# Two-layer streaming encoder on one core: more modulation vectors by selector products, and layer 0's last piece and short conv laid out anew

## The chip, the core and the metric

The program runs on one core of one Trainium2 chip, in one launch. The metric is device time in microseconds (us) of that launch. Engines are named as in the profile: PE (TensorE matmul) and PEld (its weight loads), DVE (VectorE), ACT (ScalarE), POOL (GpSimd), SP (SyncE, which here only issues transfers). Each engine runs its own list of instructions; waits between engines are semaphores.

## The reference, cut to what matters

256 tokens of width 2048 pass two layers, in float32. Each layer is

```
mod = silu(c) @ w_mod[l] + b_mod[l]            # six vectors of 2048: shift, scale, gate; twice
h = layer_norm(x) * (1 + scale_m) + shift_m
proj = h @ w_in[l]                             # 4288 columns, four head groups
y = concat(gmlp, latent attention, short conv, conformer conv) @ w_out[l]
x = layer_norm(ALPHA * x + (1 + gate_m) * y, post_mix_g[l], post_mix_b[l])
h = layer_norm(x) * (1 + scale_f) + shift_f
x = layer_norm(ALPHA * x + (1 + gate_f) * conv_ffn(h), post_ffn_g[l], post_ffn_b[l])
```

The weights w_mod, w_in, w_out, w_up and w_down are read once each; that is most of the 601 MB that the page shows as read.

## The kernel before, in words

**Tiles.** Tokens are two tiles of 128 (t0, t1; in the trace x0 and x1), the model width is 16 tiles of 128 (kt). A weight arrives as a raw tile of 1 MB (`rawp`, four buffers). Most products are done in three passes: ACT rounds the weights to a high part (`whi`, L455), DVE makes the low part (`wlo`, L456), the activations are split likewise, and PE adds high x high, high x low and low x high. The halves live in `splitp`: four buffers for high, four for low. Other products use the float32 weights as they are (`wexact`, loaded straight into buffers of `splitp` or into a slot); the trace shows two PE records for each of these. Every matmul is issued by the helper at L83.

**Modulation.** The six vectors of a layer are sums over 16 row tiles of w_mod, made on DVE: `mod_step` (L245, executed as L248 and L250) multiplies a tile by a column of silu(c) and adds it into `macc`. These steps run in the background, paced by the products (`mod_stream`, `pump`). A finished `macc` still has to be summed over its 128 partitions. For a gate this is `gate_rows` (L283). For a shift or scale there are two ways. `mod_cols` (L198) takes 128 columns of `macc` as PE's weights against one column of ones: a matmul with one output column for each of up to 16 tiles, all in float32, then one ACT instruction (L207 or L86). `mod_rows` (L220) splits `macc` into high and low parts on ACT and DVE (`mhi`, `mlo`; `halves`, L214, from the buffers of `splitp`), multiplies them by selector matrices of four columns, 512 columns at a time (`ps_row`), copies the four rows to SBUF on ACT (`mrow`, L227), transposes them on PE in four instructions (L230), and adds the bias on DVE (L232, tile `mod`). `settle` (L299) chooses: before, `mod_rows` for layer 1's shift_f and scale_f, `mod_cols` for the rest. Of layer 0's shift_f and scale_f the last 4 of 16 column tiles are summed apart, later (`LATE_KT` = 12).

**Output projections and norms.** `out_proj` (L663) serves w_out (tiles o) and w_down (tiles d). It goes over the output columns in chunks of 1024, 512 and 512. Of the last chunk the last four units of weights are held back, and `done` (L832) multiplies them for t0 and then for t1. Then it calls `before()`, which settles the shift and scale that the next norm needs (`needs`, L1499), and then `finish` for t0 (L701 yg, L704 x, L707 statistics), `second` (the norm of t0), and the same for t1 with `norm`. `first_group` (L613) then transposes the normed tile on PE (L594, ps_xT), applies scale and shift, and begins the next products with t0 alone, then t1. The tiles o_153600 and o_153610 are w_out's last chunk for t0 and t1; d_153600 and d_153610 the same for w_down of layer 0.

**Layer 0's mixers.** `by_pieces` (L1250) goes over the 16 kt in five pieces, because layer 0's own shift and scale become known piece by piece. In each, products for the groups D (conformer conv), U and V (gMLP), E (short conv's gate) are made, D in four parts between the others. After the last piece (kt 12 to 15) come `mix_d` (which queues 31 taps of a depthwise conv as background work: four ACT products and one DVE add, L910, for a tap), `mix_v` (gMLP's norm and mixing, tiles va, mixed, ya), group B with `mix_b` (the attention: tiles kvr, ps_rkv, qc, ps_sc, p, ps_pT) and group C (the short conv, tiles C_c). B and C use `wexact` throughout.

**Order.** The instructions are written in the program's order and then placed on each engine by a scheduler; the order that results is fixed when the program is built.

Of the kernel before, what the change touches and what calls it, by code (L numbers as in the profile page):

```python
# [8 lines left out]
F32R = mybir.dt.float32r  # L9
AF = mybir.ActivationFunctionType  # L10
# [3 lines left out]
P = 128  # L14
# [4 lines left out]
KT = D // P  # L19
# [35 lines left out]
def encoder_kernel(ctx: ExitStack, tc: tile.TileContext, A: dict, consts: bass.AP, out: bass.AP):  # L55
# [26 lines left out]
    def mm(o, lhsT, rhs, start, stop):  # L82
        pe.matmul(o, lhsT, rhs, start=start, stop=stop, skip_group_check=True)  # L83
# [127 lines left out]
            MOD[(l, m, k0 + j)] = cols[:, j : j + 1]  # L211
            MOD_BY[(l, m, k0 + j)] = done.ins.name

    def halves(acc, c0):  # L214
        hi = splitp.tile([P, 1024], F32R, tag="whi", name="mhi")
        lo = splitp.tile([P, 1024], F32R, tag="wlo", name="mlo")
        split((hi, lo), acc[:, c0 : c0 + 1024])
        return [(hi[:, i * 512 : (i + 1) * 512], lo[:, i * 512 : (i + 1) * 512]) for i in range(2)]

    def mod_rows(l, m, acc):  # L220

        ps = ms_tile("ps_row")
        for j, pair in enumerate(halves(acc, 0) + halves(acc, 1024)):
            for n, part in enumerate(pair):
                mm(ps[0:4, :], onesR[:, P + 4 * j : P + 4 * j + 4], part, j + n == 0, j + n == 4)
        row = tmp_tile("mrow")
        act.copy(row[0:4, :], ps[0:4, :])  # L227
        ps = ms_tile("ps_mod")
        for i in range(4):
            pe.transpose(ps[:, 4 * i : 4 * i + 4], row[0:4, i * P : (i + 1) * P], ident[0:4, 0:4])  # L230
        cols = keep.tile([P, KT], F32, name=f"mod_{l}_{m}")
        done = dve.scalar_tensor_tensor(  # L232
            out=cols.rearrange("p (i j) -> p i j", i=4),
            in0=ps[:, 0:KT].rearrange("p (i j) -> p i j", i=4),
            scalar=0.0 if m == SHIFT_F else 1.0,
            in1=bcol[l][:, m * KT : (m + 1) * KT].rearrange("p (j i) -> p i j", i=4),
            op0=ALU.add,
            op1=ALU.add,
        )
        for k in range(KT):  # L240
# [58 lines left out]
    def settle(i=0):  # L299
        l, m, acc, k0, k1 = late.pop(i)  # L300
        if m in (GATE_M, GATE_F):
            gate_rows(l, m, acc)
        elif (l, m) in ((1, SHIFT_F), (1, SCALE_F)):
            mod_rows(l, m, acc)
        else:
            mod_cols(l, m, k0, acc[:, k0 * P : k1 * P])

# [165 lines left out]
    def split(dst, src):  # L473
        hi, lo = dst[:2]
        act.copy(hi, src)  # L475
        dve.tensor_tensor(out=lo, in0=src, in1=hi.bitcast(F32), op=ALU.subtract)  # L476

    def group(w, c0, width, name, then, ntm=0, nk=2, hF=None, bg=0, spare=0, begun=None):

        ncm = (width - 512 * ntm) // P
        box = {}

        skip = 0 if begun is None else PLAIN_KT // nk

        def products(item, u):
            if u == skip:
                box["c"] = [acc_tile(f"{name}_c{i}") for i in range((ncm + 1) // 2)]
                if begun is not None:  # L490
                    for bank, part in zip(box["c"], begun):
                        act.copy(bank, part)
                box["t"] = [[acc_tile(f"{name}_t{t}{i}") for i in range(ntm)] for t in range(2)]
                box["h"] = list(hT)
            for part in (range(0, min(4, ncm)), range(4, ncm)):
                for k, (hi, lo) in enumerate(item):
                    kt = u * nk + k
                    st, sp = kt == 0, kt == KT - 1
                    for i in part:
                        o = box["c"][i // 2][:, (i % 2) * S : (i % 2 + 1) * S]  # L500
                        off = slice(i * P, (i + 1) * P)
                        first = st and i % 2 == 0
                        if lo is None:
                            mm(o, hi[:, off], hF(kt), first, sp)
                        else:
                            xh, xl = (h[:, kt % 2, :] for h in box["h"][kt // 2][:2])
                            mm(o, hi[:, off], xh, first, False)
                            mm(o, hi[:, off], xl, False, False)
                            mm(o, lo[:, off], xh, False, sp)
            for k, (hi, lo) in enumerate(item):  # L510
                kt = u * nk + k
                st, sp = kt == 0, kt == KT - 1
                for i in range(ntm):
                    off = slice(ncm * P + i * 512, ncm * P + (i + 1) * 512)
                    for t in range(2):
                        tok = slice(t * P, (t + 1) * P)
# [344 lines left out]
    def mixers(l, w_in, Y, hF=None, between=None):  # L861
# [102 lines left out]
                    func=AF.Gelu_apprx_tanh,  # L964
                )

        def mix_v(_, tps):
            ua = Y["a"]
            if l == 0:
                ga, gb = act_tile("gmlp0"), act_tile("gmlp1")  # L970
            else:
# [10 lines left out]
            va = slot("va").rearrange("p (t c) -> p t c", t=2)  # L982
            for t in range(2):
                act.activation(out=va[:, t, :], in_=tps[t][0], func=AF.Gelu_apprx_tanh)
# [5 lines left out]
            pool.memset(wT[64:128, :, 0:64], 0.0)  # L990
            for t in range(2):
# [239 lines left out]
                )  # L1231

        if hF is not None:
            return by_pieces(l, w_in, hF, between, mix_d, mix_u, mix_v, mix_b, mix_c, mix_e)
# [12 lines left out]
        run(group(w_in, C_SB, 512, f"E{l}", mix_e, nk=4, bg=STEPS[l]["E"]))  # L1247
        drain_background()

    def by_pieces(l, w_in, hF, between, mix_d, mix_u, mix_v, mix_b, mix_c, mix_e):  # L1250


        hf = lambda kt: hF[kt // 4][:, kt % 4, :]
# [49 lines left out]
        for q, (k0, nkt) in enumerate(PIECES):  # L1303
# [22 lines left out]

            turns_d = [(kt, h) for kt in range(k0, k0 + nkt) for h in range(2)]
            n = len(turns_d) // 4
            for s in range(4):
                mine = turns_d[s * n : (s + 1) * n]  # L1330
                if ("D", mine[0][0]) not in loaded:
                    load("D", mine[0][0])
                some_mods((0.3, 0.7, 1.0, 1.0)[s])
                if s == 3 and ahead[1] is not None:
                    ahead[1]()
                for kt, h in mine:
                    d_part(kt, h)
                for g in ("U", "VB", "E", "")[s] if exact else ("U", "V", "E", "")[s]:
# [3 lines left out]
                if k0 + nkt == KT:  # L1342
                    if s < 3:
                        next(mods)
                    if s > 0:
                        turns.pop(0)()
                    if s == 3:
                        turns.pop(0)()
# [270 lines left out]
```

## Time and profile before

| What | Value |
|---|---|
| Median of 3 runs | 2282.78 us (2282.72 to 2288.62) |
| Profiled execution, its own time | 2281.42 us |
| Its span, first to last instruction | 2279.7 us |
| PE, DVE, ACT busy | 98%, 78%, 48% of the span |
| Mean granted PE clock | 0.991 |
| DVE's busy tenths, layer 0's mixers | 7 to 9 |
| End of layer 0's attention and short conv, first product of w_out | 313.68 us |
| First transposes after w_out and after w_down of layer 0 | 417.94 and 1191.44 us |

A row of a timeline gives start, duration, engine, line, operation, output and inputs, and in brackets how long the engine had been idle and for whom. A row of windows gives for a stretch the busy time of PE, PEld, DVE, ACT and POOL with the count of instructions, then the granted PE clock as a fraction of full speed.

### The profile page before, as it was taken

How to read it: one execution, taken by the hardware profiler on the slowest of the kernel's cores; microseconds unless marked ns; L12 is line 12 of the kernel's file. 1: busy time of each engine (PE TensorE's matmuls, PEld its weight loads, DVE VectorE, ACT ScalarE, POOL GpSimd, SP SyncE). 2: the span in 40 equal slices, each digit the busy share in tenths (PEclk: the TensorE clock that was granted, in tenths of full speed). 3: DMA queues.
4: the chain of work that ended last, by engine and by line, in shares of the span. 5: the costliest groups of instructions: out<-in, count | busy, mean ns of one | idle time of the engine just before them, and what ended most of it. 6: DMA issues, size and time to landing. Idle time of an engine off the chain costs nothing.

```text
span 2279.7 us, 31503 instructions
## 1 busy us (share of the span) xinstructions
PE 2238.7 (98%) x12387; PEld 1934.8 (85%) x12387; DVE 1773.3 (78%) x2183; ACT 1098.2 (48%) x1644; POOL 35.1 (2%) x65
## 2 busy tenths in 40 slices
PE   7999999999999999999999999999999999999998
PEld 5788886798888888888789999889888888888886
DVE  5778988888888888988977899787676565565776
ACT  3356641354455444544454434545544454454553
POOL 0011000000000000000000000000000000000000
PEclk9999999999999999999999999999999999999999
DMA  9999699778888888898777677775666555555554
GB/s 349 385 373 359 256 328 349 249 278 314 311 307 315 314 312 327 303 346 302 273 236 254 201 242 250 271 273 177 240 240 215 192 185 197 191 185 194 187 191 148
DMA packets 228717, 605.21 MB, mean 265 GB/s; under 512 B 14660, under 2 KB 27188, under 8 KB 210900
## 3 DMA queue, kind: packets, MB, share of 16 engines
q1 hardware_dynamic: 227784, 602.30, 74.3%
q8 instruction: 97, 1.59, 0.3%
q0 software_dynamic: 784, 0.90, 0.1%
q14 instruction: 52, 0.43, 0.0%
HBM read 601.05 MB, written 2.10 MB: 265 GB/s over the span
## 4 chain that ended last, share of the span: by engine, by line
PE 88%; DVE 7%; DMA 2%; ACT 2%; issue 1%; POOL 0%; SPq 0%; DVEq 0%; ACTq 0%; POOLq 0%
PE g_c L83 22%; PE v_c L83 22%; PE d L83 20%; PE o L83 7%; PE D_c L83 3%; PE C_c L83 3%; PE B_c L83 2%; PE U_c L83 1%; PE E L83 1%; PE E_c L83 1%; DVE wlo L456 1%; PE ps_mod L83 1%; PE V L83 1%; DVE qacc L250 1%; DVE macc L250 1%
## 5 line engine op out<-in xcount | busy, mean ns | idle before, releaser
L455 ACT CAST whi<-wraw 128x1024 fp32r<-128x1024 f32 (+1 forms) x632 | 643.4, 1043 | 753.1 <-PE g_c L83 217.0
L456 DVE TENSOR_TENSOR wlo<-wraw,whi 128x1024 fp32r<-128x1024 f32 (+1 forms) x632 | 750.5, 1214 | 294.3 <-ACT whi L455 273.2
L83 PE MATMUL d<-whi,a 128*128 128x512 f32 x1344 | 390.3, 391 | 0.9 <-ACT whi L455 0.9
L250 DVE SCALAR_TENSOR_TENSOR macc<-wmod,cact,macc 128x2048 f32<-128x2048 f32 (+2 forms) x174 | 353.9, 2034 | 41.5 <-DMA wmod<-in_w_mod_dram 40.8
L83 PE MATMUL v_c<-hT,whi 128*128 128x512 f32 (+1 forms) x1456 | 343.1, 383 | 0.0
L83 PE MATMUL g_c<-hT,whi 128*128 128x512 f32 (+1 forms) x1344 | 313.5, 380 | 0.0
L83 PEld LDWEIGHTS v_c<-hT,whi 128*128 128x128 f32 x1456 | 264.6, 189 | 48.5
L83 PEld LDWEIGHTS d<-whi,a 128*128 128x128 f32 x1344 | 253.4, 189 | 54.5 <-ACT whi L455 2.2
L83 PEld LDWEIGHTS g_c<-hT,whi 128*128 128x128 f32 x1344 | 243.4, 189 | 43.5 <-DVE second L1436 0.4
L83 PE MATMUL d<-wlo,a 128*128 128x512 f32 x672 | 234.8, 392 | 1.6 <-DVE wlo L456 1.6
L83 PE MATMUL v_c<-hT,wlo 128*128 128x256 f32 x1400 | 190.7, 283 | 0.0
L83 PEld LDWEIGHTS v_c<-hT,wlo 128*128 128x128 f32 x1400 | 183.1, 191 | 6.6
L83 PE MATMUL g_c<-hT,wlo 128*128 128x256 f32 x1280 | 175.8, 283 | 0.0
L83 PEld LDWEIGHTS g_c<-hT,wlo 128*128 128x128 f32 x1280 | 168.2, 191 | 5.9
L83 PEld LDWEIGHTS d<-wlo,a 128*128 128x128 f32 x672 | 126.7, 189 | 30.1 <-DVE wlo L456 3.6
L475 ACT CAST a<-g 128x512 fp32r<-128x512 f32 x132 | 80.8, 619 | 91.1 <-PE d L83 89.4
L83 PE MATMUL o<-whi,a 128*128 128x512 f32 x384 | 111.3, 395 | 0.2 <-ACT whi L455 0.2
L476 DVE TENSOR_TENSOR a<-g,a 128x512 fp32r<-128x512 f32 x132 | 87.7, 684 | 9.2 <-ACT a L475 9.2
L250 DVE SCALAR_TENSOR_TENSOR qacc<-wmod,cact,qacc 128x1024 f32<-128x1024 f32 (+1 forms) x75 | 80.3, 1071 | 12.2 <-DMA wmod<-in_w_mod_dram 9.9
L83 PEld LDWEIGHTS o<-whi,a 128*128 128x128 f32 x384 | 72.7, 190 | 16.4 <-issue 0.7
L83 PE MATMUL D_c<-hT,whi 128*128 128x256 f32 x432 | 83.0, 292 | 2.4 <-ACT hT L475 1.6
L83 PEld LDWEIGHTS D_c<-hT,whi 128*128 128x128 f32 x432 | 69.5, 197 | 4.8 <-ACT hT L475 1.7
(370 smaller groups left out, 2619.1 us busy)
## 6 DMA issues: line engine op xcount, KB each, us to landing
wraw<-in_ffn_w_up_dram SPq DMA_DIRECT2D x168, 1024.0 KB, 5.0
wmod<-in_w_mod_dram SPq DMA_DIRECT2D x134, 1024.0 KB, 6.8
wraw<-in_ffn_w_down_dram SPq DMA_DIRECT2D x88, 1024.0 KB, 5.1
wraw<-in_w_in_dram SPq DMA_DIRECT2D x33, 1024.0 KB, 6.1
wmod<-in_w_mod_dram SPq DMA_DIRECT2D x64, 512.0 KB, 9.4
wraw<-in_w_out_dram SPq DMA_DIRECT2D x26, 1024.0 KB, 6.9
wmod<-in_w_mod_dram SPq DMA_DIRECT2D x32, 768.0 KB, 7.5
wexact<-in_w_in_dram SPq DMA_DIRECT2D x46, 512.0 KB, 7.9
```

The costliest lines, as they stand in the source:

```text
L83: pe.matmul(o, lhsT, rhs, start=start, stop=stop, skip_group_check=True)
L250: i = dve.scalar_tensor_tensor(out=acc, in0=w, scalar=col, in1=acc, op0=ALU.mult, op1=ALU.add)
L455: act.copy(hi[:, :m], r)
L456: i = dve.tensor_tensor(out=lo[:, :m], in0=r, in1=hi[:, :m].bitcast(F32), op=ALU.subtract)
L475: act.copy(hi, src)
L476: dve.tensor_tensor(out=lo, in0=src, in1=hi.bitcast(F32), op=ALU.subtract)
```

## The change

Three edits. **First,** `settle` uses `mod_rows` for every shift or scale that starts at column tile 0: layer 0's shift_f and scale_f (12 column tiles, three selector groups) and layer 1's shift_m and scale_m (16). `mod_cols` stays for the five pieces and the late four tiles. **Second,** in layer 0's last piece all of D is multiplied first; then `mix_d` queues the taps, gMLP's weights are loaded (`load_gmlp`) and transposed after U (`turn_gmlp`), the first four taps are issued with E, and two of the four `turns` (transposes of parameter rows) move behind eight taps. **Third,** in group C two of its eight units (2 and 3, kt 4 to 7) are split and done in three passes, the other six stay `wexact`.

```
     def settle(i=0):
-        elif (l, m) in ((1, SHIFT_F), (1, SCALE_F)):
-            mod_rows(l, m, acc)
+        elif k0 == 0:
+            mod_rows(l, m, acc, k1 // 4)

     def mod_rows(l, m, acc, n=4):
+        parts = [x for c0 in range(0, n * 512, 1024) for x in halves(acc, c0, min(1024, n * 512 - c0))]
+        for j, pair in enumerate(parts):
+            for i, part in enumerate(pair):
+                mm(ps[0:4, :], onesR[:, P + 4 * j : P + 4 * j + 4], part, j + i == 0, j + i == n)

     def load(u, spare=spare):      # in group()
-        return weights(w, u * nk, nk, c0, width, hF is not None, spare if u == 0 else 0)
+        return weights(w, u * nk, nk, c0, width, hF is not None and u not in passes, spare if u == 0 else 0)

     # in by_pieces()
+            if k0 + nkt == KT:
+                for kt, half in turns_d:
+                    d_part(kt, half)
+                gmlp = load_gmlp()
+                mix_d(accD, None)
+                for n, g in enumerate("UVE"):
+                    load(g, k0)
+                    next(mods)
+                    for _ in range(4 if n > 1 else 0):
+                        background.pop(0)()
+                    side(g, [(kt, loaded[(g, kt)]) for kt in range(k0, KT)], k0, nkt)
+                    if g == "U":
+                        gmlp = turn_gmlp(*gmlp)
+                    if n == 1:
+                        turns.pop(0)()
+                        turns.pop(0)()
+                drain_turns = [turns.pop(0), turns.pop(0)]
+                background[8:8] = drain_turns
+                continue
-        mix_d(accD, None)
-        mix_v(None, [[x] for x in sums["V"]])
+        mix_v(gmlp, [[x] for x in sums["V"]])
-        run(group(w_in, C_SC, 1024, f"C{l}", mix_ce, hF=hf, bg=STEPS[l]["C"]))
+        run(group(w_in, C_SC, 1024, f"C{l}", mix_ce, hF=hf, bg=STEPS[l]["C"], passes=(2, 3)))
```

What this does to the order on the engines is seen at three places. The first is DVE at the end of layer 0's w_out; x_97 is t0, `yg<-o_153600` its first step of the norm. Before:

```order
L720 BN_STATS st_o0b<-gb 128x6 x4
L722 BN_AGGR mv_o0b<-st_o0b 128x2
L724 TENSOR_SCALAR c_o_2715<-mv_o0b 128x1
L701 TENSOR_TENSOR yg<-o_153600_2725,gate_2_1980 128x512
L704 SCALAR_TENSOR_TENSOR x_97<-x_97,yg 128x512
L707 BN_STATS st_o_2227<-x_97 128x6
```

And DVE there in the changed kernel:

```order
L725 TENSOR_SCALAR c_o_2791<-mv_o0b 128x1
L477 TENSOR_TENSOR mlo<-macc,mhi 128x1024
L477 TENSOR_TENSOR mlo<-macc,mhi 128x512
L477 TENSOR_TENSOR mlo<-macc,mhi 128x1024
L477 TENSOR_TENSOR mlo<-macc,mhi 128x512
L233 SCALAR_TENSOR_TENSOR mod_3_2893<-ps_mod,bcol_106 128x4x3
L702 TENSOR_TENSOR yg<-o_153600_2801,gate_2_2034 128x512
L233 SCALAR_TENSOR_TENSOR mod_4_2917<-ps_mod,bcol_106 128x4x3
L705 SCALAR_TENSOR_TENSOR x_97<-x_97,yg 128x512
L708 BN_STATS st_o_2303<-x_97 128x6
```

Four splits and the two bias adds of the selector way (mod_3 is shift_f, mod_4 scale_f) now stand ahead of t0's norm, one of the adds inside it. The second place is PE at the same point of the program. Before, the column sums of scale_f stand ahead of nearly all of the held-back products:

```order
L83 MATMUL o_153610_2726<-wexact,ya 128x512 x2
L83 MATMUL ps_mod<-onesR,macc 128x1 x12
L83 MATMUL o_153600_2725<-wexact,yb 128x512 x4
L83 MATMUL o_153600_2725<-wexact,yc 128x512 x4
L83 MATMUL o_153600_2725<-wexact,yd 128x512 x4
L83 MATMUL o_153610_2726<-wexact,yb 128x512 x4
L83 MATMUL o_153610_2726<-wexact,yc 128x512 x4
L83 MATMUL o_153610_2726<-wexact,yd 128x512 x4
L594 MATMUL ps_xT<-cst,xn 128x128 x8
```

In the changed kernel PE has, from t0's last products on:

```order
L83 MATMUL o_153600_2801<-wexact,yd 128x512 x4
L83 MATMUL o_153610_2802<-wexact,yb 128x512 x2
L83 MATMUL o_153610_2802<-wexact,yc 128x512 x4
L83 MATMUL o_153610_2802<-wexact,yd 128x512 x4
L83 MATMUL ps_row<-mhi,onesR 4x512
L83 MATMUL ps_row<-mlo,onesR 4x512
L83 MATMUL ps_row<-mhi,onesR 4x512
L83 MATMUL ps_row<-mlo,onesR 4x512
L83 MATMUL ps_row<-mhi,onesR 4x512
L83 MATMUL ps_row<-mlo,onesR 4x512
L231 MATMUL ps_mod<-cst,mrow 128x4 x4
L83 MATMUL ps_row<-mhi,onesR 4x512
```

The selector products stand behind the last product of t1, the second vector's behind the first's transposes. At the end of layer 0's w_down the same has happened (16 `ps_row` in two eights behind d_153610 on PE; four `mlo`, mod_0, `yg<-d_153600`, mod_1 in that order on DVE). The third place is DVE in layer 0's attention, at the point where the first scores (`ps_sc`) are masked. Before:

```order
L358 TENSOR_TENSOR macc<-macc,brow 1x2048
L910 TENSOR_TENSOR convD<-convD,prodD 128x4x234
L476 TENSOR_TENSOR a<-ya,a 128x2x256
L910 TENSOR_TENSOR convD<-convD,prodD 128x4x233
L248 TENSOR_SCALAR macc<-wmod,cact 128x1536
L1150 TENSOR_SCALAR ps_sc<-ps_sc 64x4x64
```

And in the changed kernel:

```order
L359 TENSOR_TENSOR macc<-macc,brow 1x2048
L1118 TENSOR_TENSOR rope<-ps_qr_1761,qc 128x256
L911 TENSOR_TENSOR convD<-convD,prodD 128x4x232
L457 TENSOR_TENSOR wlo<-wraw,whi 128x1024 x2
L249 TENSOR_SCALAR macc<-wmod,cact 128x1536
L911 TENSOR_TENSOR convD<-convD,prodD 128x4x231
L251 SCALAR_TENSOR_TENSOR macc<-wmod,cact,macc 128x1536
L911 TENSOR_TENSOR convD<-convD,prodD 128x4x230
L1158 TENSOR_SCALAR ps_sc<-ps_sc 64x4x64
```

Two of the four low parts of group C's split units, a w_mod step and taps come ahead of the mask. From the mixing of gMLP (the third `mixed`) to the last `p` of the attention DVE's list holds, beside what is alike, 28 taps, 9 w_mod steps of 2048 columns and 8 of 1536 before, and 24 taps, 11 and 9 steps and 4 `wlo` after. On PE 31 products of B stood ahead of gMLP's mixing, now 25.

More of the change, by code (lines that the diff above doesn't have):

```diff
@@ L212, in mod_cols, with halves, mod_rows @@
             MOD_BY[(l, m, k0 + j)] = done.ins.name
[L214 to L220, printed above, removed]
+    def halves(acc, c0, width=1024):
+        hi = splitp.tile([P, 1024], F32R, tag="whi", name="mhi")[:, :width]
+        lo = splitp.tile([P, 1024], F32R, tag="wlo", name="mlo")[:, :width]
+        split((hi, lo), acc[:, c0 : c0 + width])
+        return [(hi[:, i : i + 512], lo[:, i : i + 512]) for i in range(0, width, 512)]
+    def mod_rows(l, m, acc, n=4):
         ps = ms_tile("ps_row")
-        for j, pair in enumerate(halves(acc, 0) + halves(acc, 1024)):
-            for n, part in enumerate(pair):
-                mm(ps[0:4, :], onesR[:, P + 4 * j : P + 4 * j + 4], part, j + n == 0, j + n == 4)
+        parts = [x for c0 in range(0, n * 512, 1024) for x in halves(acc, c0, min(1024, n * 512 - c0))]
+        for j, pair in enumerate(parts):
+            for i, part in enumerate(pair):
+                mm(ps[0:4, :], onesR[:, P + 4 * j : P + 4 * j + 4], part, j + i == 0, j + i == n)
         row = tmp_tile("mrow")
@@ L232, in mod_rows @@
         done = dve.scalar_tensor_tensor(
[L233 to L236, printed above, removed]
+            out=cols.rearrange("p (i j) -> p i j", i=4)[:, :, :n],
+            in0=ps[:, 0:KT].rearrange("p (i j) -> p i j", i=4)[:, :, :n],
+            scalar=0.0 if m in (SHIFT_M, SHIFT_F) else 1.0,
+            in1=bcol[l][:, m * KT : m * KT + 4 * n].rearrange("p (j i) -> p i j", i=4),
             op0=ALU.add,
@@ L239, in mod_rows @@
         )
-        for k in range(KT):
+        for k in range(4 * n):
             at = 4 * (k % 4) + k // 4
@@ L476, in split, with group @@
         dve.tensor_tensor(out=lo, in0=src, in1=hi.bitcast(F32), op=ALU.subtract)
-    def group(w, c0, width, name, then, ntm=0, nk=2, hF=None, bg=0, spare=0, begun=None):
+    def group(w, c0, width, name, then, ntm=0, nk=2, hF=None, bg=0, spare=0, begun=None, passes=()):
         ncm = (width - 512 * ntm) // P
@@ L965, in mix_u, with load_gmlp @@
                 )
-        def mix_v(_, tps):
-            ua = Y["a"]
+        def load_gmlp():
             if l == 0:
@@ L981, in mix_v, with turn_gmlp @@
             )
-            va = slot("va").rearrange("p (t c) -> p t c", t=2)
-            for t in range(2):
-                act.activation(out=va[:, t, :], in_=tps[t][0], func=AF.Gelu_apprx_tanh)
+            return ga, gb
+        def turn_gmlp(ga, gb):
             wT = slot("wT")[:, :512].rearrange("p (h i) -> p h i", h=4)
@@ L990, in mix_v @@
             pool.memset(wT[64:128, :, 0:64], 0.0)
+            return ga, gb, wT
+        def mix_v(loaded, tps):
+            ua = Y["a"]
+            ga, gb, wT = loaded or turn_gmlp(*load_gmlp())
+            va = slot("va").rearrange("p (t c) -> p t c", t=2)
+            for t in range(2):
+                act.activation(out=va[:, t, :], in_=tps[t][0], func=AF.Gelu_apprx_tanh)
             for t in range(2):
@@ L1233, in mixers @@
         if hF is not None:
-            return by_pieces(l, w_in, hF, between, mix_d, mix_u, mix_v, mix_b, mix_c, mix_e)
+            return by_pieces(l, w_in, hF, between, mix_d, mix_u, mix_v, mix_b, mix_c, mix_e, load_gmlp, turn_gmlp)
         phase(l, "U")
@@ L1248, in mixers, with by_pieces @@
         drain_background()
-    def by_pieces(l, w_in, hF, between, mix_d, mix_u, mix_v, mix_b, mix_c, mix_e):
+    def by_pieces(l, w_in, hF, between, mix_d, mix_u, mix_v, mix_b, mix_c, mix_e, load_gmlp, turn_gmlp):
         hf = lambda kt: hF[kt // 4][:, kt % 4, :]
@@ L1337, in by_pieces @@
                     d_part(kt, h)
-                for g in ("U", "VB", "E", "")[s] if exact else ("U", "V", "E", "")[s]:
+                for g in ("U", "VB" if exact else "V", "E", "")[s]:
                     load(g, k0)
@@ L1341, in by_pieces @@
                     side(g, [(kt, loaded[(g, kt)]) for kt in range(k0, k0 + nkt)], k0, nkt)
[L1342 to L1348, printed above, removed]
-        mix_d(accD, None)
-        mix_v(None, [[x] for x in sums["V"]])
+        mix_v(gmlp, [[x] for x in sums["V"]])
         phase(l, "B")
```

## The prediction

> **What bounds the kernel now.** I read the page first, then the windows and timelines of the three places that the change touches.
>
> ```profile
> span 2279.7 us, 31503 instructions
> PE 2238.7 (98%) x12387; PEld 1934.8 (85%) x12387; DVE 1773.3 (78%) x2183; ACT 1098.2 (48%) x1644; POOL 35.1 (2%) x65
> PE 88%; DVE 7%; DMA 2%; ACT 2%; issue 1%; POOL 0%; SPq 0%; DVEq 0%; ACTq 0%; POOLq 0%
> ```
>
> PE is busy for all but 41 us and makes 88% of the chain that ended last. So a product taken from PE is worth its PE time, and whatever lets PE wait is added. The norms are where PE comes nearest to waiting. Timelines of DVE and of PE at the end of layer 0's w_out:
>
> ```profile
> 406.91 0.69 DVE L701 TENSOR_TENSOR yg<-o,gate 128x512 f32<-128x512 f32 x1 [8.79 <-PE o L83]
> 407.64 0.69 DVE L704 SCALAR_TENSOR_TENSOR x<-x,yg 128x512 f32<-128x512 f32 x1
> 417.21 0.69 DVE L701 TENSOR_TENSOR yg<-o,gate 128x512 f32<-128x512 f32 x1 [0.23 <-PE o L83]
> 406.71 3.60 PE L83 MATMUL o<-wexact,yb 128*128 128x512 f32 x8
> 413.58 3.60 PE L83 MATMUL o<-wexact,yd 128*128 128x512 f32 x8
> 417.94 1.36 PE L594 MATMUL ps_xT<-cst,xn 128*128 128x128 f32 x8 [0.77 <-ACT xn L86]
> 429.79 0.66 PE L594 MATMUL ps_xT<-cst,xn 128*128 128x128 f32 x4 [0.79 <-ACT xn L86]
> ```
>
> DVE begins t0's norm at 406.91, when t0's products are done. PE multiplies t1's until 413.58 + 3.60 = 417.18. The norm's ten microseconds lie under those products, and PE waits 0.77. The same at the end of layer 0's w_down:
>
> ```profile
> 1180.02 0.69 DVE L701 TENSOR_TENSOR yg<-d,gate 128x512 f32<-128x512 f32 x1 [1.97 <-PE d L83]
> 1180.74 0.69 DVE L704 SCALAR_TENSOR_TENSOR x<-x,yg 128x512 f32<-128x512 f32 x1
> 1190.47 0.39 PE L83 MATMUL d<-whi,a 128*128 128x512 f32 x1
> 1191.44 1.36 PE L594 MATMUL ps_xT<-cst,xn 128*128 128x128 f32 x8 [0.58 <-ACT xn L86]
> ```
>
> Here PE ends at 1190.47 + 0.39 = 1190.86 and waits 0.58.
>
> **Selector products: what is removed.** The column sums of the four vectors, the first block from the timeline, the others from windows that hold one block of them or the products behind it. The last two rows are products after an idle stretch, behind the one-column sums of one of the five pieces: their place in PE's timeline, then their window.
>
> ```profile
> 1039.20 1.70 PE L83 MATMUL ps_mod<-onesR,macc 128*128 128x1 f32 x14
> 341.11:344.15 3.04, 3.04 (x29) 3.04 (x28) 2.36 (x3) 1.64 (x3) 0.00 (x0) 1.00 1.00 397
> 344.15:348.58 4.43, 4.43 (x15) 3.48 (x15) 3.55 (x3) 1.07 (x2) 0.00 (x0) 0.61 0.89 329
> 393.73:396.33 2.60, 2.60 (x26) 2.60 (x24) 2.56 (x5) 0.00 (x0) 0.00 (x0) 1.00 1.05 406
> 1041.77:1043.92 2.15, 2.15 (x22) 2.15 (x20) 0.00 (x0) 0.05 (x1) 0.00 (x0) 1.00 0.77 265
> 1043.92:1048.35 4.43, 4.43 (x15) 3.51 (x14) 3.33 (x3) 2.01 (x3) 0.00 (x0) 0.61 0.58 224
> 1118.80:1122.29 3.49, 3.49 (x34) 3.49 (x32) 3.49 (x5) 1.88 (x3) 0.00 (x0) 1.00 0.69 284
> 1122.29:1126.49 4.20, 4.20 (x13) 3.30 (x13) 2.38 (x3) 2.15 (x3) 0.00 (x0) 0.59 0.78 252
> 82.56 1.23 PE L83 MATMUL D_c<-hT,whi 128*128 128x256 f32 x4 [1.62 <-ACT hT L475]
> 82.56:88.36 5.80, 5.44 (x23) 5.15 (x24) 5.73 (x6) 0.95 (x2) 0.00 (x0) 0.50 1.05 385
> ```
>
> Layer 0's two vectors take 3.04 + 2.60 = 5.6 us, layer 1's 1.70 + 2.15 + 3.49 = 7.3. Behind three of the four blocks the granted clock is about 0.6 for 4.2 to 4.4 us: 0.39 x 4.43 = 1.7, again 1.7, and 0.41 x 4.20 = 1.7 lost. One-column matmuls thus cost more than their own time. Removed in all: 5.6 + 1.7 = 7.3 at w_out, 7.3 + 3.4 = 10.7 at w_down.
>
> **Selector products: what is added.** Layer 1's shift_f goes this way already:
>
> ```profile
> 776.16 0.40 PE L83 MATMUL ps_row<-mhi,onesR 128*4 128x512 f32 x1
> 776.39 0.39 PE L83 MATMUL ps_row<-mlo,onesR 128*4 128x512 f32 x1
> 780.14 0.57 ACT L227 COPY mrow<-ps_row 4x512 f32<-4x512 f32 x1
> 780.77 0.41 PE L230 MATMUL ps_mod<-cst,mrow 4*128 4x4 f32 x4
> 781.32 0.17 DVE L232 SCALAR_TENSOR_TENSOR mod<-ps_mod,bcol 128x16 f32<-128x16 f32 x1
> 773.74 1.05 ACT L475 CAST mhi<-macc 128x1024 fp32r<-128x1024 f32 x1
> 776.78 1.22 DVE L476 TENSOR_TENSOR mlo<-macc,mhi 128x1024 fp32r<-128x1024 f32 x1
> ```
>
> One selector product costs 776.39 - 776.16 = 0.23; from mrow to the end of the bias add it is 781.49 - 780.14 = 1.35. PE's own 28 products and 16 transposes, about 6.4 + 1.6 = 8 us, would be less than what goes. But the order decides. On DVE the bias add of shift stands ahead of t0's yg, that of scale ahead of t0's second step; both need `ps_row`, which stands on PE behind t1's last product. Queued behind the waiting add are t0's whole norm, then t1's; waiting for that is PE, whose next work is ps_xT.
>
> At w_out, counted from PE's last product: six selector products 1.4, mrow and transposes 1.2, the second six 1.4, and 0.1 + 1.35 to its add, 5.4 in all. From L704 to ps_xT it was 417.94 - 407.64 = 10.3. So ps_xT comes 5.4 + 10.3 = 15.7 behind the last product, where it was 0.76: 14.9 more. At w_down there are eight products each, 1.85 and 1.85, and the high parts can be cast only as the last two held-back units free their buffers, which puts two casts of 1.05 ahead of the first mrow; I take 6.5. With 1191.44 - 1180.74 = 10.7 that is 17.2 against 0.58: 16.6 more. The selector path alone lies between 4.5 and 7.5 at each place.
>
> PE then starts after some ten idle microseconds. Nearest is the window at 82.56 above, which follows an idle 1.6 us behind one-column sums: clock 0.50 for 5.8 us, 2.9 lost. At w_down I count that in full, since the group there goes to t0 first and t1 is seen to be waited for at w_out only. At w_out the wait of 0.79 at 429.79 takes some back: 2.1. Bounds 0 and 3.5 each. The Trainium skill (TensorE: Matmul & The Clock Gate, "What's actually happening") has half rate released after about 3.4 us of sustained work, an estimate of 1.7 us per norm, with which the forecast would be some 2 us lower; the 5.8 us at 0.50 speak for the longer.
>
> Sum: w_out 14.9 + 2.1 - 7.3 = +9.7; w_down 16.6 + 2.9 - 10.7 = +8.8. Together +18.5. The DVE splits (3.7 and 4.9 us at 1.22 for 1024 columns) lie in DVE's idle 8.79 at w_out and in the path counted above at w_down.
>
> **Last piece and short conv.** Rows of group C, group E and B, DVE's groups in the attention, and the last wait in it:
>
> ```profile
> 255.48 11.39 PE L83 MATMUL C_c<-hF,wexact 128*128 128x256 f32 x52
> 266.75 0.63 PE L1181 MATMUL ps_pT<-cst,p 128*128 128x128 f32 x3
> 175.97 5.76 PE E L83 x48
> 200.91 17.86 PE L83 MATMUL B_c<-hF,wexact 128*128 128x256 f32 x82
> 287.94 0.63 PE L1181 MATMUL ps_pT<-cst,p 128*128 128x128 f32 x4 [0.38 <-DVE p L1172]
> 200.44:288.06 87.62, 86.93 (x399) 73.37 (x398) 85.06 (x97) 57.95 (x145) 1.63 (x3) 0.96 0.80 293
> L456 DVE TENSOR_TENSOR wlo<-wraw,whi 128x1024 fp32r<-128x1024 f32 (+1 forms) x632 | 750.5, 1214 | 294.3 <-ACT whi L455 273.2 <-PE g_c L83 11.4 <-PE v_c L83 1.9
> L250 DVE SCALAR_TENSOR_TENSOR macc<-wmod,cact,macc 128x2048 f32<-128x2048 f32 (+1 forms) x17 | 35.6, 2093 | 0.3 <-DMA wmod<-in_w_mod_dram 0.3
> L910 DVE TENSOR_TENSOR convD<-convD,prodD 128x1012 f32<-128x1012 f32 (+27 forms) x28 | 32.1, 1146 | 0.3 <-ACT prodD L909 0.2
> ```
>
> An exact product costs PE (266.75 - 255.48) / 26 = 0.43, three passes 3 x 5.76 / 48 = 0.36. Two units are 2 x 2 x 8 = 32 such products: 2.3 us off PE. The reordering takes no work from PE. But DVE is busy 85.06 of 87.62 us between gMLP's mixing and the last p, and PE waits for that p: the two engines are level here. DVE's list gains 4 wlo x 1.21, 2 + 1 w_mod steps (about 2.1 each) and loses 4 taps x 1.15: 4.9 + 6.3 - 4.6 = +6.6. It can start earlier by six products of B, 6 x 17.86 / 41 = 2.6, and 85.06 of 87.62 leaves at most another 2.6 of idle to take up. The last p then comes 1.4 to 4.0 later, with one more product of C behind it (39 against 38, 0.4). I take +2.0; bounds -2.3 (PE alone) and +6 (w_mod loads that come late as well, the window's DMA share being 0.80). The early gMLP loads are four more issues on SP ahead of V's weights, which by the piece's 28 us of products have slack; if not, at most 2.
>
> **Sum.** 18.5 + 2.0 = +20.5 on 2281.4, the profiled execution's own time: 2301.9. The median, 2282.8, lies 1.4 higher; I say 2302.
>
> **Rivals.** *DVE congestion is small* (the forecast's own low side): PE's 2.3 us are gained and the attention keeps up, 18.5 - 2.3, so 2298; for it, 2.6 us of idle and the taps begun early; against it, the added steps. 0.2. *The short conv costs 8*: w_mod tiles late, 2308; 0.15. *One norm only is exposed*, say because at w_down the sums come through in time: +9.7 there against -10.7 + 4.6 of selector work, 2281 + 9.7 - 6.1 + 2 = 2287, within the bound; the order speaks against it. 0.06. *The sums hide, the kernel is faster*: PE meets no wait, as when DVE took yg ahead of the waiting add. Then PE's 13.0 + 5.0 of sums and slow clock become 8, and with the short conv's 2.3 the time is 2269. It decides by whether the first selector product runs before t1's products end. DVE's rows of before came in the order's sequence at both norms, which speaks against it. The Trainium skill (TensorE: Matmul & The Clock Gate, "Architectural detail") calls DVE strict FIFO; no row of before tests it. 0.05.
>
> **Chances and range.** Forecast 0.54. A measurement here can tell about 0.3%, 7 us. Slower 0.54 + 0.2 + 0.15 = 0.89, same 0.06, faster 0.05. The range is the forecast with the selector path (3 down, 2 up in all), the clock (5 down, 2 up) and the short conv (4 either way), not all at once: 2290 to 2310.
>
> **What would show it.** In the profile after, at both norms: yg of t0 behind the bias add, about 3 us after PE's last product; an idle PE of about 10 us with ps_xT released by xn; a clock near 0.5 behind it. No stretch at 0.6 near 341, 1044 and 1122. At the last p, 288.06 becomes 289 to 292. If ps_row runs before t1's products, or PE's wait before ps_xT stays under 2 us, the prediction is wrong.

## The result, and the profile after

The changed kernel takes 2306.32 us (median of 5 runs, 2304.67 to 2308.32), the kernel before 2283.2 in runs taken with them. The ratio is 1.0095, with a 95% interval of 1.0081 to 1.0109: 23.1 us slower by the medians, beyond the 0.3% that the prediction took a measurement to tell. The forecast was 2302, the range 2290 to 2310. The first two lines of the page, after:

```profile
span 2304.0 us, 31454 instructions
PE 2232.4 (97%) x12343; PEld 1923.3 (83%) x12343; DVE 1786.0 (78%) x2199; ACT 1108.7 (48%) x1655; POOL 36.9 (2%) x65
```

PE has less to do, 2232.4 us against 2238.7, and the span is 24.3 us longer: its idle time grows from 41.0 to 71.6 us, so the loss is waiting. Where it enters is read from the start or end of the same product in PE's timelines of both kernels:

| Place on PE | Before, us | After, us | Later by |
|---|---|---|---|
| First product of the attention's ps_kn | 245.43 | 253.55 | 8.1 |
| First product of w_out | 313.68 | 320.77 | 7.1 |
| Last product of w_out for t1, its end | 417.18 | 417.92 | 0.7 |
| First transposes behind it | 417.94 | 433.44 | 15.5 |
| First product of w_down | 935.66 | 952.73 | 17.1 |
| Last product of w_down for t1, its end | 1190.86 | 1198.64 | 7.8 |
| First transposes behind it | 1191.44 | 1215.53 | 24.1 |
| First ps_kn of layer 1 | 1350.23 | 1373.35 | 23.1 |
| End of the span | 2279.7 | 2304.0 | 24.3 |

Three places lose time (the attention and the two norms), and the two output projections give some of it back. First the norm behind w_out: DVE's timeline of the changed kernel, ACT's, then PE's.

```profile
414.58 0.69 DVE L477 TENSOR_TENSOR mlo<-macc,mhi 128x512 fp32r<-128x512 f32 x1 [11.90 <-issue]
418.01 1.99 DVE L477 TENSOR_TENSOR mlo<-macc,mhi 128x1024 fp32r<-128x1024 f32 x2 [2.74 <-PE o L83]
420.43 0.17 DVE L233 SCALAR_TENSOR_TENSOR mod<-ps_mod,bcol 128x12 f32<-128x12 f32 x1 [0.42 <-PE ps_mod L231]
420.51 0.68 DVE L702 TENSOR_TENSOR yg<-o,gate 128x512 f32<-128x512 f32 x1
422.98 0.17 DVE L233 SCALAR_TENSOR_TENSOR mod<-ps_mod,bcol 128x12 f32<-128x12 f32 x1 [1.79 <-PE ps_mod L231]
423.07 0.68 DVE L705 SCALAR_TENSOR_TENSOR x<-x,yg 128x512 f32<-128x512 f32 x1
```

ACT casts the high parts of the second and third split:

```profile
412.81 0.62 ACT L476 CAST mhi<-macc 128x512 fp32r<-128x512 f32 x1 [16.12 <-PE o L83]
416.24 1.04 ACT L476 CAST mhi<-macc 128x1024 fp32r<-128x1024 f32 x1 [2.82 <-PE o L83]
```

And PE:

```profile
405.74 3.60 PE L83 MATMUL o<-wexact,yd 128*128 128x512 f32 x8
...
414.32 3.60 PE L83 MATMUL o<-wexact,yd 128*128 128x512 f32 x8
...
433.44 1.97 PE L595 MATMUL ps_xT<-cst,xn 128*128 128x128 f32 x8 [10.50 <-ACT xn L86]
```

PE ends t1's last product at 417.92. t0's products are finished at 405.74 + 3.60 = 409.34, but t0's norm stands behind the splits and the adds in DVE's list. DVE stands at the second of the four splits (`mlo`) until 414.58 and at the third until 418.01: their high parts are cast only when products of o on PE release them, and the third split itself is released by such a product. Then DVE waits 0.42 us at the bias add of shift_f and 1.79 at that of scale_f, until 422.98. So it is first the splits that hold DVE, not the adds. With the splits alone ahead of the norm, L705 would have come at about 420.0 + 0.7 = 420.7, an estimate from these rows; the adds account for the last 2.3 us. No run moves one without the other.

Only behind the second add does t0's norm go on (L705 at 423.07), 10.4 us ahead of ps_xT, as many as before (10.3). PE waits 10.50 of them. In both kernels the norm is the same string of instructions; before, its second step came 9.5 us ahead of PE's end (407.64), now 5.15 us behind it. At w_down it stands 6.1 us behind PE's end (1204.76 - 1198.64), in a timeline of both engines. There DVE stands idle 10.99 us ahead of the splits, which run until 1202.04; the first add then waits for nothing, the second 1.85:

```profile
1197.04 5.08 DVE L477 TENSOR_TENSOR mlo<-macc,mhi 128x1024 fp32r<-128x1024 f32 x4 [10.99 <-ACT mhi L476]
...
1198.25 0.39 PE L83 MATMUL d<-whi,a 128*128 128x512 f32 x1
...
1202.04 0.17 DVE L233 SCALAR_TENSOR_TENSOR mod<-ps_mod,bcol 128x16 f32<-128x16 f32 x1
...
1204.66 0.17 DVE L233 SCALAR_TENSOR_TENSOR mod<-ps_mod,bcol 128x16 f32<-128x16 f32 x1 [1.85 <-PE ps_mod L231]
1204.76 0.69 DVE L705 SCALAR_TENSOR_TENSOR x<-x,yg 128x512 f32<-128x512 f32 x1
...
1215.53 1.97 PE L595 MATMUL ps_xT<-cst,xn 128*128 128x128 f32 x8 [10.90 <-ACT xn L86]
```

The third place is new in kind. Timelines of both engines in the attention, before and then after: PE's short conv, the wait and ps_qn, and the DVE rows that release ps_rkv.

```profile
222.07 0.48 DVE L1054 TENSOR_SCALAR kvr<-B_c,pm 128x256 f32<-128x256 f32 x1
...
222.62 9.21 PE L83 MATMUL C_c<-hF,wexact 128*128 128x256 f32 x28
...
229.69 0.48 DVE L1076 TENSOR_SCALAR dgB<-cst,rr 128x128 f32<-128x128 f32 x2
...
231.66 0.59 PE L83 MATMUL ps_rkv<-dgB,onesR 128*128 128x256 f32 x2
...
233.24 5.45 PE L83 MATMUL ps_qn<-qg,wq 128*128 128x256 f32 x24
```

```profile
223.82 5.43 PE L83 MATMUL C_c<-hF,wexact 128*128 128x256 f32 x24
...
226.77 0.48 DVE L1062 TENSOR_SCALAR kvr<-B_c,pm 128x256 f32<-128x256 f32 x1
...
234.30 0.48 DVE L1084 TENSOR_SCALAR dgB<-cst,rr 128x128 f32<-128x128 f32 x2
...
234.83 1.22 PE L83 MATMUL ps_rkv<-dgB,onesR 128*128 128x256 f32 x2 [5.58 <-DVE dgB L1084]
...
237.98 7.76 PE L83 MATMUL ps_qn<-qg,wq 128*128 128x256 f32 x24
```

Before, DVE came to kvr, the attention's first step, at 222.07, and dgB was ready at 230.2, while PE still had 1.6 us of the short conv's first unit. Now kvr is at 226.77, dgB at 234.30 to 234.78, and PE has run out of that unit at 229.25. It waits 5.58 us, and the 24 products of ps_qn behind it take 7.76 us instead of 5.45.

That PE did not wait here before is in part chance. In the profile of before its granted clock was 0.50 in this stretch (the first of these two rows, a window), so that 28 records of the short conv took 9.21 us; in e3, an experiment below that leaves the last piece as it was, they take 6.29 (the second row), and PE then waits 1.84 us for dgB.

```profile
222.00:228.00 6.00, 6.00 (x17) 4.92 (x18) 5.95 (x9) 5.82 (x15) 0.00 (x0) 0.50 1.00 415
```

```profile
221.62 6.29 PE L83 MATMUL C_c<-hF,wexact 128*128 128x256 f32 x28
```

So at full clock the kernel before would wait for dgB as well, an estimate of some 1.8 us from e3; the change moves dgB from 229.69 to 234.30. What that costs is better read from the times of e1 and e2 than from this one pair of profiles. Windows of the changed kernel show the granted clock behind this wait and behind the two norms (the column of PE's clock is the third from the end):

```profile
234.83:238.00 3.17, 3.17 (x7) 1.68 (x7) 3.17 (x4) 1.36 (x4) 0.00 (x0) 0.50 1.02 429
238.00:242.00 4.00, 4.00 (x11) 3.19 (x11) 3.90 (x3) 0.73 (x2) 0.00 (x0) 0.50 0.32 79
242.00:246.00 4.00, 4.00 (x18) 3.51 (x17) 0.86 (x2) 2.76 (x7) 0.00 (x0) 0.91 0.58 224
433.44:436.00 2.56, 2.56 (x11) 2.37 (x12) 2.46 (x6) 2.56 (x6) 0.90 (x1) 0.50 0.00 0
436.00:439.00 3.00, 3.00 (x23) 3.00 (x23) 3.00 (x6) 1.58 (x5) 0.09 (x1) 0.79 0.00 0
1215.53:1218.50 2.97, 2.97 (x13) 2.78 (x14) 2.87 (x7) 2.97 (x7) 0.92 (x1) 0.50 0.02 6
1218.50:1222.00 3.50, 3.50 (x32) 3.50 (x31) 3.50 (x6) 1.86 (x5) 0.00 (x0) 0.94 0.00 0
320.77:360.00 39.23, 38.85 (x170) 31.54 (x169) 34.03 (x36) 15.26 (x20) 0.00 (x0) 1.00 0.93 341
360.00:417.92 57.92, 57.92 (x170) 31.68 (x170) 38.08 (x41) 7.30 (x8) 0.00 (x0) 1.00 0.85 313
```

Behind the attention's wait the clock costs 3.17 x 0.50 + 4.00 x 0.50 + 4.00 x 0.09 = 3.9 us, behind the norms 1.9 and 1.7. All through w_out it is 1.00: the stretch at 0.61 behind the one-column sums is gone.

### The profile page after: what moved, and what is told of

Its sections match the earlier page's. It is cut to its first block, busy times and chain, and to the rows that moved or that the text cites. A ratio compares the mean times of both kernels' runs of the same rounds, so it can differ in the third digit from the quotient of the medians.

```text
span 2304.0 us, 31454 instructions
## 1 busy us (share of the span) xinstructions
PE 2232.4 (97%) x12343; PEld 1923.3 (83%) x12343; DVE 1786.0 (78%) x2199; ACT 1108.7 (48%) x1655; POOL 36.9 (2%) x65
## 4 chain that ended last, share of the span: by engine, by line
PE 87%; DVE 7%; DMA 2%; ACT 2%; issue 2%; POOL 0%; DVEq 0%; SPq 0%; ACTq 0%; POOLq 0%
PE g_c L83 22%; PE v_c L83 21%; PE d L83 19%; PE o L83 6%; PE C_c L83 4%; PE D_c L83 4%; DVE wlo L457 1%; PE U_c L83 1%; PE B_c L83 1%; PE E_c L83 1%; PE U L83 1%; PE V L83 1%; PE E L83 1%; DVE macc L251 1%; DVE qacc L251 1%
## 5 line engine op out<-in xcount | busy, mean ns | idle before, releaser
L83 PEld LDWEIGHTS o<-whi,a 128*128 128x128 f32 x384 | 72.0, 188 | 16.6 <-ACT whi L456 1.1
L1397 DVE SCALAR_TENSOR_TENSOR u<-g,pf,u 128x254 f32<-128x254 f32 (+1 forms) x176 | 73.5, 480 | 0.0
```

The costliest lines, as they stand in the source:

```text
L1397: dve.scalar_tensor_tensor(out=u[:, sh:], in0=x[:, : S - sh], scalar=col(k, j), in1=u[:, sh:], op0=ALU.mult, op1=ALU.add)
```

## The experiments

Each differs from one of the two kernels by the edits named. e1 to e4 have 10 runs each, e5 to e8 11. The first four were timed beside the kernel before at 2283.21 (median of 31 runs), the last four beside it at 2285.55 (29 runs); only the ratio compares across the two sets.

| Run | Median, us | Ratio to before (95%) |
|---|---|---|
| changed kernel | 2306.32 | 1.0095 (1.0081 to 1.0109) |
| e1, without the first edit | 2290.01 | 1.0025 (1.0014 to 1.0036) |
| e2, second edit only | 2290.56 | 1.0024 (1.0013 to 1.0035) |
| e3, third edit only | 2283.81 | 0.9997 (0.9985 to 1.0010) |
| e4, vectors settled behind t0's norm | 2287.62 | 1.0013 (1.0003 to 1.0023) |
| e5, sums ahead of the held-back products | 2284.19 | 0.9989 (0.9981 to 0.9998) |
| e6, the same, first edit only | 2278.91 | 0.9968 (0.9958 to 0.9979) |
| e7, second edit without its taps | 2285.38 | 1.0001 (0.9991 to 1.0011) |
| e8, e6 and third edit | 2281.82 | 0.9983 (0.9972 to 0.9993) |

**Taking the edits apart: e1, e2, e3.** The edits, from the changed kernel for e1, from the kernel before for e3; e2 is e1 without `passes`. e3 also gets the parameter `passes` and its use in `load`, as shown under the change:

```
 e1      def settle(i=0):
-        elif k0 == 0:
+        elif (l, m) in ((1, SHIFT_F), (1, SCALE_F)):
             mod_rows(l, m, acc, k1 // 4)
 e2
-        run(group(w_in, C_SC, 1024, f"C{l}", mix_ce, hF=hf, bg=STEPS[l]["C"], passes=(2, 3)))
+        run(group(w_in, C_SC, 1024, f"C{l}", mix_ce, hF=hf, bg=STEPS[l]["C"]))
 e3
-        run(group(w_in, C_SC, 1024, f"C{l}", mix_ce, hF=hf, bg=STEPS[l]["C"]))
+        run(group(w_in, C_SC, 1024, f"C{l}", mix_ce, hF=hf, bg=STEPS[l]["C"], passes=(2, 3)))
```

> The changed kernel with the first edit undone (one-column sums for the four vectors, as before); the last piece and the two split units stay. Theory (the norms' waits belong to the selector products' place, the 5.6 us wait ahead of ps_rkv and the slow clock behind it to the other two edits): no idle near 10 us at the two norms, PE still idle 5 to 6 us ahead of ps_rkv, first product of w_out about 7 us later than before; 2283.2 + 7 = 2290, 2288 to 2292. Rival, the forecast's size of this term (+2.0): 2285. Rival, these two edits cost nothing and all of the 23 us is the norms': 2281 to 2283.

> The kernel before with the second edit only (the last piece). Theory (six more taps stand on DVE ahead of the attention's kvr): PE idles 5 to 6 us ahead of ps_rkv, and without the third edit's 2.3 us off PE the kernel takes 2291, 2289 to 2293. Rival, the four low parts of the third edit are what holds DVE up: no wait ahead of ps_rkv, 2282 to 2284.

> The kernel before with the third edit only (two units of the short conv in three passes). Theory (the attention's wait is decided ahead of kvr, where this edit adds nothing to DVE): PE's 2.3 us are gained, 2281, 2280 to 2282. Rival, the forecast's reason (DVE and PE are level up to the last p, four low parts of 1.21 us come late): the last p 2 to 3 us later, 2284 to 2286.

PE's timelines of e1 (the first two rows) and of e2 and e3 at the same wait:

```profile
234.21 1.22 PE L83 MATMUL ps_rkv<-dgB,onesR 128*128 128x256 f32 x2 [5.59 <-DVE dgB L1084]
...
425.47 1.97 PE L595 MATMUL ps_xT<-cst,xn 128*128 128x128 f32 x8 [1.21 <-ACT xn L86]
```

```profile
234.58 1.22 PE L83 MATMUL ps_rkv<-dgB,onesR 128*128 128x256 f32 x2 [5.58 <-DVE dgB L1084]
```

```profile
229.75 0.67 PE L83 MATMUL ps_rkv<-dgB,onesR 128*128 128x256 f32 x2 [1.84 <-DVE dgB L1076]
```

e1 comes out at its theory's 2290, with the first product of w_out at 319.75, 6.1 us later than before: with the one-column sums back, PE waits 1.21 us at w_out's norm instead of 10.50, and still 5.59 ahead of ps_rkv. e2 has the wait without the third edit; its 2290.56 fits 2291, and the rival, which blamed the third edit's low parts, would have had neither the wait nor the time. (In e2's profiled execution, 3.2 us above its median, the first product of w_out comes at 324.72, 11.0 later than before; what gives part of that back isn't traced. e3's 1.84 us is no mark of its edit: e6 below, which leaves the short conv alone, has 1.86.) So the second edit costs about 7 us by the medians, 5.5 by the ratio (3 to 8), and the first the other 16 of the 23 us (2306.3 - 2290.0).

e3 does not decide as hoped. By its time it can't: the interval, 0.9985 to 1.0010, is 2279.8 to 2285.5 and holds both the theory's 2281 and part of the rival's 2284 to 2286. In the profiles its first product of w_out comes 3.1 us earlier (310.57 against 313.68), the theory's place and sign, but the profile of before had lost some 3 us to a slow clock in the attention, so these 3.1 are not the edit's alone. Behind it the lead is gone: from the first transposes behind w_out to the first product of w_down e3 takes 519.7 us against 517.7 before (516.9 to 519.3 in the other profiles); what gives it back isn't shown. The later last p that the rival names isn't seen: its products end at 284.16 instead of 288.57. e1 and e2 differ by the third edit as well, and their medians by 0.5 us: its 2.3 us off PE show in no time here.

**The order at the norm: e4.**

```
-                if before is not None:
-                    before()
                 for t in range(2):
+                    if t == 1 and before is not None:
+                        before()
                     finish(t, state["ps"], c0)
                     (norm if t == 1 or then is None else second)(t)
```

> The changed kernel with one move: shift and scale are settled behind the norm of t0 instead of ahead of it, so that DVE takes t0's norm before the waiting bias adds. Nothing else differs; the selector products still stand behind the last product of t1. Theory (DVE's order makes the wait): t0's norm lies under t1's products again, the idle 10.5 and 10.9 us ahead of ps_xT fall below 1, the selector path of 5 and 6 us stays between the last product and ps_xT; 2306.3 - 21.4 - 2 of slow clock = 2283, 2281 to 2286. Rival, the wait is set by the selector path and the transposes' own inputs and not by DVE's order: 2300 or more.

The timeline of DVE and PE in e4 at the end of w_out:

```profile
409.46 0.69 DVE L702 TENSOR_TENSOR yg<-o,gate 128x512 f32<-128x512 f32 x1 [6.70 <-PE o L83]
...
414.41 3.60 PE L83 MATMUL o<-wexact,yd 128*128 128x512 f32 x8
...
420.56 0.17 DVE L233 SCALAR_TENSOR_TENSOR mod<-ps_mod,bcol 128x12 f32<-128x12 f32 x1
...
421.29 0.69 DVE L702 TENSOR_TENSOR yg<-o,gate 128x512 f32<-128x512 f32 x1
...
424.33 1.68 PE L595 MATMUL ps_xT<-cst,xn 128*128 128x128 f32 x8 [1.19 <-ACT xn L86]
```

DVE takes t0's yg at 409.46, three of the four splits only from 417.34 on, the bias add at 420.56 and t1's yg behind it. The idle 10.50 has become 1.19, at w_down 10.90 has become 1.18, and 18.7 us are back (2306.3 to 2287.6). The selector products stand where they stood on PE; what differs is DVE's order. So DVE's order made the wait, and the rival falls; splits and adds moved together, so the run doesn't tell their shares apart. The time is a little over its band of 2281 to 2286: the selector path that stays behind the last product is longer than assumed, 424.33 - 418.01 = 6.3 us to ps_xT at w_out and 8.1 (1187.27 to 1195.33) at w_down, 14.4 against 11.

**Sums without either cost: e5, e6.** The selector products can't stand earlier on PE while their halves wait for the buffers of the held-back units (the casts at 412.81 and 416.24 above). Halves in small tiles, and settling ahead of the held-back products:

```
+    def in_tmp(acc, c0):
+        hi = tmpp.tile([P, 512], F32R, tag="tmp", name="mhi")
+        lo = tmpp.tile([P, 512], F32R, tag="tmp", name="mlo")
+        split((hi, lo), acc[:, c0 : c0 + 512])
+        return hi, lo
     def mod_rows(l, m, acc, n=4):
+        if (l, m) in WITH_NORM:
+            parts = (in_tmp(acc, c0) for c0 in range(0, n * 512, 512))
...
     # in out_proj's done()
+                if last and before is not None:
+                    before()
                 for t in range(2):
                     for item, u in state["tail"]:
...
-                if before is not None:
-                    before()
```

e5 is the changed kernel with this, e6 the kernel before with this and the first edit.

> The changed kernel with one cause taken away: the high and low parts of the four vectors go to small tiles of 512 columns instead of the buffers that the held-back units occupy, and the vectors are settled ahead of the held-back products. The selector products then stand among t0's last products, the bias adds ahead of t0's yg without a wait. Theory (what costs is that the sums stand behind t1's last product; the sums themselves are cheaper): no idle above 1.5 us at the two norms, no selector path behind the last product; against the run with the settling behind t0's norm (2287.6) another 5 + 6 us of path go, but 28 products and 16 transposes, about 8 us, stay as PE work inside it: 2278, 2275 to 2282. Rival, splits of 512 columns and their sums disturb the last chunk (ACT and DVE late for the held-back products): 2285 or more.

> The kernel before with only this: the four vectors by selector products, through the small tiles, settled ahead of the held-back products. Neither the last piece nor the split units. Theory: the one-column sums and the slow clock behind them (measured: 6.4 us at w_out, 9.3 at w_down) go, some 8 us of selector work come, nothing waits: 2283.2 - 15.7 + 8 = 2275.5, 2273 to 2279. Rival, the sums of before were mostly hidden or their clock comes back elsewhere: 2281 to 2284.

PE of e6: two rows of the sums at w_out, then the first transposes behind w_out and behind w_down.

```profile
393.50 0.39 PE L83 MATMUL ps_row<-mlo,onesR 128*4 128x512 f32 x1 [1.06 <-DVE mlo L486]
...
398.92 0.41 PE L240 MATMUL ps_mod<-cst,mrow 4*128 4x4 f32 x4
...
419.47 1.36 PE L604 MATMUL ps_xT<-cst,xn 128*128 128x128 f32 x8 [0.85 <-ACT xn L86]
...
1188.60 1.36 PE L604 MATMUL ps_xT<-cst,xn 128*128 128x128 f32 x8 [0.68 <-ACT xn L86]
```

The selector products now run among t0's held-back ones, and ps_xT follows the last product of t1 after 0.85 and 0.68 us. e6 is the fastest kernel here: 0.9968, 7.3 us below the kernel before (2285.55 x 0.0032), where 7.7 were expected. So the first edit's selector products are the cheaper way, by 7 us; as they were placed they cost 16. e5 shows the price of the place directly: 1.0095 - 0.9989 of 2283, 24 us. e5's ratio of 0.9989 is 2280.7 on the first set's 2283.2, inside its band; its norms wait 1.71 and 0.67 us, the first a little over the 1.5 expected, and it keeps the 5.58 us ahead of ps_rkv. That it lies 0.0021 above e6, 4.8 us, agrees with what the second and third edit cost in e1.

**The taps: e7.** The second edit without its four taps beside group E:

```
-                    for _ in range(4 if n > 1 else 0):
+                    for _ in range(0):
                         background.pop(0)()
```

> The kernel before with the second edit, but without its four taps beside group E (2290.6 with them). Theory (the taps pushed ahead of kvr make the wait): DVE comes to dgB four taps of 1.15 us earlier, the idle 5.6 us ahead of ps_rkv falls to 1 or less and the slow clock behind it goes: 2284, 2282 to 2287. Rival, it is the w_mod steps that this piece leaves for later: the wait stays above 3 us, 2288 or more.

The timeline of PE and DVE in e7 where the changed kernel waits 5.58 us:

```profile
224.82 5.62 PE L83 MATMUL C_c<-hF,wexact 128*128 128x256 f32 x18
...
227.84 0.48 DVE L1084 TENSOR_SCALAR dgB<-cst,rr 128x128 f32<-128x128 f32 x2
...
230.28 0.59 PE L83 MATMUL ps_rkv<-dgB,onesR 128*128 128x256 f32 x2
...
231.86 5.45 PE L83 MATMUL ps_qn<-qg,wq 128*128 128x256 f32 x24
```

dgB is made at 227.84 instead of 234.30, ps_rkv starts without a wait and ps_qn takes 5.45 again. The time is that of the kernel before, 1.0001: the taps were the cause, and the rest of the second edit is worth nothing that can be told (the interval is some 2.3 us either way). The w_mod steps that the rival blamed are no fewer: from the first step of the vector in work, twelve of them run ahead of dgB in e7, in the changed kernel and before alike.

**Both together: e8.** e6 with e3's line.

> The kernel with the four vectors by selector products ahead of the held-back products, and the third edit with it (two units of the short conv in three passes), without the last piece's new layout. Theory (the two are independent; the third edit alone measured no difference): the same as the run with the sums only, 2275.5, 2273 to 2279. Rival, the 2 to 3 us that the third edit gained up to w_out stay once the norms are clean: 2273.

0.9983 against e6's 0.9968; on the first set's 2283.2 that is 2279.3, at the upper end of the theory's band. The intervals overlap, so whether the third edit costs some 3 us here or nothing stays open; that it adds a gain (the rival's 2273) isn't what the runs show.

## Why the prediction was right

It forecast 2302 and a slower kernel at 0.89; measured are 2306.3. By its own steps, from the profiled executions:

- **The wait at w_out**, +14.9: the first transposes come 433.44 - 417.92 = 15.5 us behind the last product instead of 0.76, +14.8. The path was as laid out: 5.15 us to L705 (5.4 in the forecast), then 10.4 (10.3). One reading on the way was wrong: the DVE splits were to lie in DVE's idle time, but three of the four came late (414.58 to 420.00) and held t0's norm before any add did. That the size came out all the same is luck in this part: the selector path on PE happened to end later than the splits.
- **The wait at w_down**, +16.6: 16.9 us instead of 0.58, +16.3. e4 shows that DVE's order, splits and adds together, is the cause of both, by taking it away.
- **The sums removed**, 7.3 and 10.7: from the first product of w_out to the last 97.2 us instead of 103.5, 6.4; from that of w_down 245.9 instead of 255.2, 9.3. A little less than forecast. The slow clock behind the sums is a matter of the single run: behind the fourth block, where the profile of before showed none, e7 has it in PE's timeline, where eight records take 6.72 us instead of 3.60. The forecast's sum was made on one execution, in which one of the four was missing.

```profile
399.21 6.72 PE L83 MATMUL o<-wexact,yb 128*128 128x512 f32 x8
```

- **The slow clock behind the idle**, 2.1 and 2.9: the windows above give 1.9 and 1.7. Of the two lengths that were weighed, 5.8 us at half rate from the nearest row or about 3.4 us of sustained work by the Trainium skill (TensorE: Matmul & The Clock Gate, "What's actually happening"), the norms fit the second: if the mixed windows are 0.50 at first and 1.00 then, half rate lasted 2.56 + 1.26 = 3.8 us and 2.97 + 0.42 = 3.4. The term was sized by the wrong one of the two; it is a small one. Behind the attention's wait half rate lasted 7.9 us (below), which fits neither.
- **Last piece and short conv**, +2.0: here the size was wrong. It measures +7.1 in the profiles (first product of w_out) and +6.8 in e1's median (5.7 by its ratio, 3.2 to 8.2), at or beyond the stated upper bound of +6. The step that failed: the cost was taken from DVE's total between gMLP's mixing and the last p, as a late last p, with the head start of 2.6 us set against it. But PE doesn't wait for a total. It waits for kvr and dgB, which come early in that list, and what counts is what stands ahead of *them*: the taps, 20 instead of 14 between mix_d and dgB, at 1.15 us (16 in e7). The six had lain behind dgB. And a wait of 5.58 us costs 9.5, because the clock falls behind it. The last p is 5.9 us late (294.50 against 288.57), outside the 1 to 4 us named for it. e2 and e7 show this cause. The 2.3 us that were counted as taken off PE show in no time (e3, e1 against e2, e8 against e6). The rival "the short conv costs 8" had the amount right and the reason wrong (no w_mod tile was late; the wait is named by dgB).

The sum by measured terms: 14.8 + 1.9 - 6.4 = 10.3 (9.7 forecast), 16.3 + 1.7 - 9.3 = 8.7 (8.8), 7.1 (2.0), 26.1 in all; the profiles differ by 24.3, the medians by 23.1. Of the difference, 1.0 us is a wait of layer 1's group B for a low part (1.16 us in the profile of before, 0.19 after); the rest isn't traced to a place.

Of the rivals, "the sums hide" had its condition right (it needs the first selector product ahead of the end of t1's products) and e6 meets it: the kernel is then faster, by 7 us, not by the 12 that the rival gave (2281.4 to 2269). Of those, 2.3 belong to the third edit, which e6 leaves out, and the sums with their slow clock measured 15.7 us (6.4 + 9.3) instead of 18.0: 15.7 - 8 = 7.7 against the 7.3 of e6.

## What to carry to other kernels

Cheaper work on the bottleneck engine pays only where its results' consumers stand: splits and adds that wait for PE's last products, put ahead of a norm in DVE's list, turned 10 us of hidden norm into 10 us of idle PE, twice. Ask of every instruction that a change moves ahead of another on the same engine when its input is ready, and look for the buffer that keeps the input late (here the halves shared buffers with the held-back weights). Background work that is pushed forward beside one group can come out ahead of the next critical step; count what stands ahead of that step, not the total, and add the slow clock behind a PE wait to its price. Before a pair of profiles is compared place by place, look at the granted clock in both: a slow stretch in one can hide a wait that is there at full clock.

## What the runs showed of the hardware

For how long the granted clock is 0.50 after an idle stretch did not follow the length of the idle: behind 10.5 and 10.9 us it lasted 3.4 to 3.8 us, behind 5.58 us in the attention 3.17 + 4.00 + 0.72 = 7.9 us, and in two other runs at that place, from windows at 0.50 and 0.64, 6.7 (e1) and 6.0 (e4). Nor does it always fall: at the same place it was 1.00 behind 1.84 us of idle in e3 (231 to 245) and 0.50 behind 1.86 in e6 (231 to 236). And one-column sums don't always bring the clock down: the block at 393 of the profile before was followed by products at full speed, the same block in e7 by products at nearly half; the short conv behind the attention's one-column sums ran at 0.50 in the profile of before (222 to 228) and at 1.00 in that of e3.
